# Mixture of experts in the order of token counts, with two-pass down products for the smallest four

## Chip, cores and metric

The kernel runs on one core of a Trainium2 chip. The metric is the device time of one execution in microseconds (us). Three executions of the kernel before gave 1408.19 to 1408.69, median 1408.42.

## What is computed

A decoder trunk of two layers on 256 tokens of 1024 channels, in float32. Layer 0 is a pooling mixer and a dense SwiGLU; layer 1 is a gated DeltaNet and a top-2-of-8 mixture of expert SwiGLUs, each with a hidden width of 3584. The change is within the experts alone:

```python
top_vals, top_idx = lax.top_k(logits, TOP_K)
top_w = jax.nn.softmax(top_vals, axis=-1)
gates = jnp.sum(jax.nn.one_hot(top_idx, N_EXPERTS) * top_w[..., None], axis=1)
for e in range(N_EXPERTS):
    y = swiglu(t, w_gate[e], w_up[e], w_down[e])
    out = out + gates[:, e:e + 1] * y
```

`swiglu` is `(silu(x @ w_gate) * (x @ w_up)) @ w_down`. Run with its drawn inputs, the reference sends 53, 51, 58, 82, 64, 88, 44 and 72 tokens to experts 0 to 7.

## The kernel before

**Splitting.** Every float32 operand is split into a rounded part and a remainder: ScalarE (ACT) casts the rounded part (`whi`, `xgh`, `th`), VectorE (DVE) subtracts it from the source to get the remainder (`wlo`, `xgl`, `tl`). A product is three TensorE (PE) matmuls that add into one PSUM bank: hi by hi, hi by lo and lo by hi.

**Weights.** The experts' weights lie in memory in units of 1 MB (`in_moe`, 42 units per expert, in the order of use). The SyncE queue (SP) loads them into a ring of 16 buffers (`raw`, `raw_s`, `raw_t`); each unit is split in two halves by `half`, with four buffers each for `whi` and `wlo`.

**Jobs.** `expert_steps` writes the jobs out: for each expert seven chunks of 512 hidden columns, each with eight gate and up jobs (6 matmuls of 512 columns each) and four down jobs (6 matmuls each, in `down_mm`) for the chunk before. `moe_pass` runs them: ahead of job i it issues the split of job i+3 (`ahead`), then the job's matmuls, then what hangs on it: `turn` (transposes the 128x512 hidden tile and splits it into `th` and `tl`), `opened` (silu), `gated` (the product with the up half) and `put` (copies the finished rows and writes them to memory by an indirect DMA). Each engine keeps the order in which its instructions were written, since `Lane.__getattr__` (line 200) records them; so nearly every row of the profile has line 200, and the tile names tell the rows apart.

**Tokens.** `choose` builds one-hot matrices `Sp` for two experts of 128 rows each from their ranks `rf`, and `gather` multiplies the tokens with them, 8 groups of 4 matmuls of 256 columns, each group followed by two copies out of PSUM (`xgh`, `xgl`). This is done for a pair of experts at a time, between the jobs of the expert ahead. `opening` is the start of the stage: it computes the first gate product on all tokens while the router's `pick` and `ranks` run on DVE. If an expert has more than 128 tokens, a second pass (`moe_pass(1)`) follows; the test for it stands at the end (lines 1685 and 1686).

Of the kernel before, what the change touches and what calls it, by code (L numbers as in the profile page):

```python
# [52 lines left out]
TURN = 4  # L53
SWAP = 9
# [157 lines left out]
def trunk(ctx: ExitStack, tc, x, gcol, win, prm, bc, cst, eye, pre, moe, out):  # L212
# [1020 lines left out]
    state, sel, xg, yps = {}, {}, {}, {}  # L1233
# [25 lines left out]
    m1, m2, ed, den, w1, w2 = [sm(n_, 1) for n_ in ("m1", "m2", "ed", "den", "w1", "w2")]  # L1259
# [4 lines left out]
    cmi = cmi[:, :1]  # L1264
# [43 lines left out]
    def ranks():  # L1308

        prk = ms_bank([P, 2, 8])  # L1310
        pe.matmul(prk[:, 0, :], ber, mk[:, 0, :], start=True, stop=True)
        pe.matmul(prk[:, 1, :], ber, mk[:, 1, :], start=True, stop=False)
        pe.matmul(prk[:, 1, :], onr, mk[:, 0, :], start=False, stop=True)
        dve.scalar_tensor_tensor(rf, prk, 1.0, mk.bitcast(F32), op0=ALU.add, op1=ALU.mult)

        pn = ms_bank([P, 8])
        for tt in range(2):
            pe.matmul(pn, onr, mk[:, tt, :], start=tt == 0, stop=tt == 1)
        return pn

    def most(pn):

        cmx = mp.tile([P, 1], F32, name="cmx")
        dve.tensor_reduce(cmx, pn, axis=AX.X, op=ALU.max)
        dve.tensor_copy(cmi, cmx)
# [14 lines left out]
    def choose(pr_):  # L1340
        Sp = state["mp"].tile([P, 2, 2, P], F32R, name="Sp", bufs=1)
        for tt in range(2):
            for k in range(2):
                dve.tensor_scalar(Sp[:, tt, k, :], iota[:, :P], rf[:, tt, 2 * pr_ + k:2 * pr_ + k + 1], None,
                                  op0=ALU.is_equal)
        state["Sp", pr_] = Sp
        for k in range(2):
            xg[2 * pr_ + k] = [None, None]

    def gather(pr_, kc, lo_eng=None, bank_=None):  # L1350
        if kc % 4 == 0:
            t = xg_tiles(kc // 4)
            for k in range(2):
                xg[2 * pr_ + k][kc // 4] = t
        pg = (bank_ or ms_bank)([P, 2, 256])
        for i, src in enumerate((hh, hl)):
            for tt in range(2):
                pe.matmul(pg[:, i, :], src[:, tt, kc * P:(kc + 1) * P],
                          state["Sp", pr_][:, tt].rearrange("p a b -> p (a b)"), start=tt == 0, stop=tt == 1)
        for i in range(2):  # L1360
            (dve.tensor_copy if i and lo_eng else act.copy)(xg[2 * pr_][kc // 4][i][:, kc % 4, :], pg[:, i, :])

    def back(e):
        pst = ms_bank([P, 2, P])
        for tt in range(2):
            pe.matmul(pst[:, tt, :], state["Sp", e // 2][:, tt, e % 2, :], idr, start=True, stop=True)
# [3 lines left out]
    def where(e):  # L1370

        pw = ms_bank([P, 8])
        for tt in range(2):
            pe.matmul(pw, state["Sp", e // 2][:, tt, e % 2, :], tid[:, tt, :], start=tt == 0, stop=tt == 1)
        spare = econ[:, 6:7]
        dve.scalar_tensor_tensor(spare, pw[:, e:e + 1], 0.0, econ[:, 3:4], op0=ALU.is_equal, op1=ALU.mult)
        dve.tensor_tensor(slot[:, e:e + 1], spare, pw[:, e:e + 1], op=ALU.add)

    def put(e, q):
        if q == 0:  # L1380
            state["put"] = state["rows"].tile([P, D], F32, name="rows", bufs=2)
        act.copy(state["put"][:, HQ[q]], yps[e][q])
        if q == 1:
            pool.indirect_dma_start(kept_rows, bass.IndirectOffsetOnAxis(ap=slot[:, e:e + 1], axis=0), state["put"], None)
# [12 lines left out]
    def opened(pg):  # L1397
        hm = row_tile()
        act.activation(hm, pg, AF.Silu)
        return hm  # L1400

    def gated(hm, pu_):
        dve.tensor_mul(hm, hm, pu_)
# [8 lines left out]
    def hidden_T(hm, spare):  # L1412
# [7 lines left out]
    def gate_pick():  # L1420

        ps_ = ms_bank([P, 512])
        for i in range(2):
            for tt in range(2):
                pe.matmul(ps_, state["Sp", 0][:, tt, 0, :], state["first"][i][tt], start=i == tt == 0, stop=i == tt == 1)
# [3 lines left out]
    def last_mm(e, c, part):  # L1429

        y, (th, tl), (hi, lo) = yps[e], state["hid", e, c], part
        for q in range(2):
            for a, b in ((th, hi), (tl, hi), (th, lo)):
# [272 lines left out]
```

## Time and profile before

| | |
|---|---|
| median of 3 runs | 1408.42 us |
| the profiled execution | 1407.77 us |
| span of its profile, first to last instruction | 1405.8 us |
| PE busy | 1384.8 us, 99% of the span |
| DVE busy | 1177.8 us, 84% |
| ACT busy | 1004.0 us, 71% |
| memory read | 420.11 MB |
| expert stage | from about 419 us to 1393 us of the span |

Times in the rows are us from the start of the span. A matmul's duration is from its first read to its modelled end; the engine starts the next one earlier, so the distance between two starts is what a matmul costs.

### The profile page before, as it was taken

The numbers are of one execution on the slowest core, as the hardware profiler recorded it, in microseconds if no ns is written. First come the engines' busy times: TensorE is split into PE (matmuls) and PEld (weight loads), VectorE is DVE, ScalarE is ACT, GpSimd is POOL, SyncE is SP. The second block draws the span as 40 slices with busy tenths as digits, with TensorE's granted clock in tenths as the row PEclk, the third lists the DMA queues.
The fourth block names the chain that finished last, engine by engine and source line by source line (L and its number), as shares of the span: only waits on it lengthen the run. The fifth ranks groups of instructions, "written<-read, shape, count | busy, mean of one in ns | idle before, by whom it ended". The sixth has DMA issues, their size and how long they took to land.

```text
span 1405.8 us, 19741 instructions
## 1 busy us (share of the span) xinstructions
PE 1384.8 (99%) x7399; PEld 1186.5 (84%) x7399; DVE 1177.8 (84%) x1438; ACT 1004.0 (71%) x1322; POOL 66.3 (5%) x73
## 2 busy tenths in 40 slices
PE   8999999999999999999999999999999999999996
PEld 8999998989988888888888888888888888888875
DVE  5655556687888999998899999899999989999996
ACT  5544445753566777878877887887887788778775
POOL 0000001121330000000000000000000000000001
PEclk9999999999999999999999999999999999999998
DMA  9465552633159999999999999899999999997880
GB/s 381 156 219 193 180 180 113 263 114 122 65 205 420 364 374 371 397 376 365 357 375 377 378 390 378 332 385 376 372 377 382 368 341 383 375 368 298 334 353 32
DMA packets 61123, 428.24 MB, mean 305 GB/s; under 512 B 6880, under 2 KB 7136, under 8 KB 10592
## 3 DMA queue, kind: packets, MB, share of 16 engines
q1 hardware_dynamic: 59584, 422.75, 78.1%
q0 software_dynamic: 1008, 3.67, 0.7%
q8 instruction: 59, 0.97, 0.3%
q10 hardware_dynamic: 432, 0.53, 0.1%
q14 instruction: 40, 0.33, 0.1%
HBM read 420.11 MB, written 6.82 MB: 304 GB/s over the span
## 4 chain that ended last, share of the span: by engine, by line
PE 94%; DVE 3%; ACT 1%; issue 1%; POOL 0%; DMA 0%; POOLq 0%; SPq 0%; DVEq 0%; ACTq 0%
PE gu L200 59%; PE y L200 21%; PE ya L200 9%; DVE wlo L200 2%; PE yq L200 2%; PE ms L200 1%; PE tp L200 1%; PE gs L200 1%; ACT whi L200 0%; DVE h L200 0%; DMA h<-in_x 0%; DVE xl L200 0%; ACT xh L200 0%; DVE raw L200 0%; POOL raw L200 0%
## 5 line engine op out<-in xcount | busy, mean ns | idle before, releaser
L200 DVE TENSOR_TENSOR wlo<-raw,whi 128x1024 fp32r<-128x1024 f32 x345 | 417.1, 1227 | 92.5 <-ACT whi L200 81.9
L200 DVE TENSOR_TENSOR wlo<-raw_s,whi 128x1024 fp32r<-128x1024 f32 x378 | 456.4, 1223 | 40.6 <-ACT whi L200 22.0
L200 ACT CAST whi<-raw_s 128x1024 fp32r<-128x1024 f32 x378 | 396.5, 1056 | 81.2 <-PE gu L200 45.4
L200 ACT CAST whi<-raw 128x1024 fp32r<-128x1024 f32 x346 | 359.4, 1053 | 110.0 <-PE gu L200 65.2
L200 PE MATMUL gu<-whi,xgh 128*128 128x512 f32 x896 | 355.6, 397 | 0.0
L200 PE MATMUL gu<-wlo,xgh 128*128 128x512 f32 x896 | 349.5, 390 | 0.5 <-DVE wlo L200 0.5
L200 PE MATMUL gu<-whi,xgl 128*128 128x512 f32 x896 | 349.6, 390 | 0.0
L200 PEld LDWEIGHTS gu<-whi,xgl 128*128 128x128 f32 x896 | 168.2, 188 | 36.6
L200 PEld LDWEIGHTS gu<-wlo,xgh 128*128 128x128 f32 x896 | 168.4, 188 | 34.2 <-DVE wlo L200 1.3
L200 PEld LDWEIGHTS gu<-whi,xgh 128*128 128x128 f32 x896 | 168.3, 188 | 32.9
L200 PE MATMUL y<-whi,th 128*128 128x512 f32 x440 | 171.4, 390 | 0.0
L200 PE MATMUL y<-wlo,th 128*128 128x512 f32 x440 | 171.3, 389 | 0.0
L200 PE MATMUL y<-whi,tl 128*128 128x512 f32 x440 | 135.5, 389 | 0.0
L200 PEld LDWEIGHTS y<-whi,tl 128*128 128x128 f32 x440 | 82.6, 188 | 17.2
L200 PEld LDWEIGHTS y<-wlo,th 128*128 128x128 f32 x440 | 82.6, 188 | 16.7
L200 PEld LDWEIGHTS y<-whi,th 128*128 128x128 f32 x440 | 82.6, 188 | 16.8
L200 PE MATMUL gu<-xh,wlo 128*128 128x256 f32 x320 | 90.0, 281 | 0.8 <-DVE wlo L200 0.8
L200 PE MATMUL gu<-xh,whi 128*128 128x256 f32 x320 | 90.1, 281 | 0.1
L200 PE MATMUL gu<-xl,whi 128*128 128x256 f32 x320 | 89.9, 281 | 0.0
L200 PEld LDWEIGHTS gu<-xh,wlo 128*128 128x128 f32 x320 | 61.3, 192 | 1.0 <-DVE wlo L200 1.0
L200 PEld LDWEIGHTS gu<-xh,whi 128*128 128x128 f32 x320 | 60.2, 188 | 0.7 <-ACT whi L200 0.3
L200 PEld LDWEIGHTS gu<-xl,whi 128*128 128x128 f32 x320 | 60.1, 188 | 0.3
(375 smaller groups left out, 1650.8 us busy)
## 6 DMA issues: line engine op xcount, KB each, us to landing
raw_s<-in_moe SPq DMA_DIRECT2D x189, 1024.0 KB, 6.7
raw<-in_moe SPq DMA_DIRECT2D x126, 1024.0 KB, 6.7
raw<-in_pre SPq DMA_DIRECT2D x56, 1024.0 KB, 5.0
raw_t<-in_moe SPq DMA_DIRECT2D x20, 1024.0 KB, 6.6
rows<-AB SPq DMA_DIRECT2D x2, 1024.0 KB, 5.5
raw<-rows SPq DMA_DIRECT2D x2, 1024.0 KB, 7.3
gbc<-in_bc SPq DMA_DIRECT2D x3, 512.0 KB, 7.8
h<-in_x SPq DMA_DIRECT2D x2, 512.0 KB, 3.9
```

What stands on the lines that cost most here:

```text
L200: r = f(*a, **k)
```

## The change

Expert 0 stays first; the other seven follow by falling token count, and their weights are loaded from unit numbers that are read into registers (`first_unit`). Experts 0 and 1 of this order run as before. Then a test on `fit`, the larger of two numbers, twice the count at the fifth place and the largest count of all, chooses one of two programs for the remaining six: if `fit` is at most 128, the last four experts have 64 rows each and share one `choose` and one `gather`, their hidden tile has 64 rows, and its transpose is stored as one tile of 128 columns, 64 rounded and 64 remainders. One matmul of this tile with `whi` and one with `wlo` then give the product's two parts in rows 0 to 63 and 64 to 127, which `put` adds. The other program is the old one for six experts, with the test for a second pass at its end.

```diff
+FEW, SLIM = 4, 64
     def ranks():
+        pn = ms_bank([P, 8])
+        for tt in range(2):
+            pe.matmul(pn, onr, mk[:, tt, :], start=tt == 0, stop=tt == 1)
...
+        dve.memset(key[:, 0:1], 1.0e6)
+        dve.scalar_tensor_tensor(key[:, 1:], pn[:, 1:], float(NE), iota[:, P + 1:], op0=ALU.mult, op1=ALU.add)
+        dve.tensor_tensor(ge, key[:, None, :].to_broadcast([P, 8, 8]), key[:, :, None].to_broadcast([P, 8, 8]), op=ALU.is_ge)
+        dve.tensor_reduce(place, ge, axis=AX.X, op=ALU.add)
...
         dve.scalar_tensor_tensor(rf, prk, 1.0, mk.bitcast(F32), op0=ALU.add, op1=ALU.mult)
+        sorted_(rf)
+        yield
...
+        dve.scalar_tensor_tensor(fit, some[:, NE - FEW:NE - FEW + 1], float(P // SLIM), top, op0=ALU.mult, op1=ALU.max)
...
     def hidden_T(hm, spare, n=P):
         tp = gu_bank((P, 4, P))
         for k in range(4):
-            pe.transpose(tp[:, k, :], hm[:, k * P:(k + 1) * P], C("ident"))
+            pe.transpose(tp[:, k, :n], hm[:n, k * P:(k + 1) * P], C("ident")[:n, :n])
+        if n < P:
+            state["side"] = 1 - state.get("side", 0)
+            th = pair(True)[0] if spare else state["tmp"].tile([P, 4, P], F32R, name=("th", "tl")[state["side"]], bufs=1)
+            split(th[:, :, :n], th[:, :, n:], tp[:, :, :n])
+            return th, None
...
             pe.matmul(y[q], th[:, fc, :], hi[:, HQ[q]], start=st, stop=False)
-            pe.matmul(y[q], th[:, fc, :], lo[:, HQ[q]], start=False, stop=False)
-        for q in qs:
+            pe.matmul(y[q], th[:, fc, :], lo[:, HQ[q]], start=False, stop=sp_ and tl is None)
+        for q in qs if tl is not None else ():
             pe.matmul(y[q], tl[:, fc, :], hi[:, HQ[q]], start=False, stop=sp_)
...
+        n, r, y = width(e), state["put"], yps[e][q]
+        if n == P:
+            act.copy(r[:, HQ[q]], y)
+        else:
+            act.copy(r[:n, HQ[q]], y[n:2 * n])
+            dve.tensor_add(r[:n, HQ[q]], r[:n, HQ[q]], y[:n])
...
-                        after(at + (3, 5)[q], put, e, q)
+                        after(at + (3, 3 if e == 1 else 5)[q], put, e, q)
...
+                if (e, c) == (2, 0) and not block:
+                    after(len(jobs) - 3, turn, *prev)
+                    down(*prev)
+                    prev, cut = None, len(jobs)
...
+            if start:
+                choose(range(2, 4))
+                ahead(start)
+                for kc in range(KC):
+                    gather(range(2, 4), kc, dve)
+                    if kc % 4 == 3:
+                        ahead(start + 1 + kc // 4)
...
+        fv = nc.values_load(fit[0:1, 0:1], min_val=0, max_val=2 * T)
+        with tc.If(fv <= P) as arm:
+            fresh()
+            units.clear()
+            steps_ = expert_steps(block, FEW)
+            run(cut, len(steps_[0]))
+        with arm.Else():
...
-            if i == len(jobs) - 20 and block == 0:
-                tc.mark_branch_hint_location("rest", "LikelyTaken", [mybir.EngineType.PE, mybir.EngineType.DVE,
...
-    rv = nc.values_load(cmi[0:1, 0:1], min_val=0, max_val=T)
-    with tc.If(rv > P, label="rest"):
-        moe_pass(1)
```

The order of instructions at three places follows.

**PE, the down jobs.** Before, one job of any expert (`y_4744` and `y_4745` are the two banks of the result):

```order
L200 MATMUL y_4744<-whi,th 128x512
L200 MATMUL y_4744<-wlo,th 128x512
L200 MATMUL y_4745<-whi,th 128x512
L200 MATMUL y_4745<-wlo,th 128x512
L200 MATMUL y_4744<-whi,tl 128x512
L200 MATMUL y_4745<-whi,tl 128x512
```

Now, one job and the first row of the next, in one of the last four experts:

```order
L203 MATMUL y_10065<-whi,th 128x512
L203 MATMUL y_10065<-wlo,th 128x512
L203 MATMUL y_10066<-whi,th 128x512
L203 MATMUL y_10066<-wlo,th 128x512
L203 MATMUL y_10065<-whi,th 128x512
```

The two matmuls with `tl` are gone. The gate and up jobs keep their six.

**ACT, where expert 1 ends.** Before, the copies of its rows stand among the splits for expert 2:

```order
L200 CAST whi<-raw_s_6748 128x1024
L200 COPY rows<-y_5772 128x512
L200 CAST whi<-raw_s_6748 128x1024
L200 CAST whi<-raw 128x1024
L200 COPY rows<-y_5773 128x512
L200 CAST whi<-raw 128x1024
```

Now:

```order
L203 CAST whi<-raw 128x1024 x3
L203 COPY rows<-y_5798 128x512
L203 COPY rows<-y_5799 128x512
L1692 TENSOR_LOAD cmi
L1693 COMPARE_AND_BRANCH
L203 CAST whi<-raw_s_6640 128x1024
L203 CAST xgh_6646<-ms 128x256 x4
L203 CAST whi<-raw_s_6640 128x1024
L203 CAST xgh_6680<-ms 128x256 x4
L203 CAST whi<-raw_s_6710 128x1024 x2
```

Both copies, the load of the tested number and the branch now stand ahead of the first split of expert 2 and of its gather, on every engine; SP has issued the loads up to here and goes on by itself.

**DVE, the router's ranks in the opening.** Before:

```order
L200 SCALAR_TENSOR_TENSOR rf<-ms,mk 128x16
L200 TENSOR_SCALAR Sp<-iota,rf 128x128 x4
L200 TENSOR_REDUCE cmx<-ms 128x1
L200 CAST cmi<-cmx 128x1
L200 TENSOR_TENSOR wlo<-raw,whi 128x1024
L200 TENSOR_TENSOR tl<-gu,th 128x512
```

Now, up to the split that follows the one-hot matrices:

```order
L203 MEMSET raw 128x1
L203 SCALAR_TENSOR_TENSOR raw<-ms,iota 128x7
L203 TENSOR_TENSOR raw<-raw 128x64
L203 TENSOR_REDUCE raw<-raw 128x8
L203 TENSOR_TENSOR raw<-raw,iota 128x64
L203 SCALAR_TENSOR_TENSOR rf<-ms,mk 128x16
L203 TENSOR_TENSOR raw<-raw,rf 128x64 x2
L203 TENSOR_REDUCE rf<-raw 128x16
L203 TENSOR_SCALAR Sp<-iota,rf 128x128 x4
L203 TENSOR_TENSOR wlo<-raw,whi 128x1024
```

Seven small operations and a memset come ahead of `Sp`. Behind this `wlo`, and ahead of `tl`, fifteen more stand where two stood: those of `ranks` after its first `yield`.

## Rows read from the trace of the kernel before

**Rows 1.** The page: busy us, share of the span, instructions.

```profile
PE 1384.8 (99%) x7399; PEld 1186.5 (84%) x7399; DVE 1177.8 (84%) x1438; ACT 1004.0 (71%) x1322; POOL 66.3 (5%) x73
```

**Rows 2.** Stretches: window; length, busy us of engines, PE's clock, DMA share, GB/s.

```profile
550.00:600.00 50.00, 50.00 (x228) 41.35 (x227) 46.25 (x43) 40.97 (x44) 1.55 (x1) 1.00 1.00 392
1300.00:1350.00 50.00, 49.76 (x225) 40.80 (x224) 47.43 (x44) 39.32 (x42) 0.00 (x0) 1.00 0.88 359
```

**Rows 3.** Waits between 460 and 1380 us: total us, times, longest.

```profile
DVE wlo L200 <- ACT whi L200: 37.9, 123, 1.2
PE gu L200 <- DVE wlo L200: 0.5, 2, 0.2
```

**Rows 4.** Timeline of POOL, the writes of finished rows: start, duration, idle before.

```profile
690.27 1.35 POOL L200 DMA_INDIRECT rows<-rows,cmi  x1 [120.32 <-ACT rows L200]
808.22 1.36 POOL L200 DMA_INDIRECT rows<-rows,cmi  x1 [116.59 <-ACT rows L200]
930.12 1.36 POOL L200 DMA_INDIRECT rows<-rows,cmi  x1 [120.54 <-ACT rows L200]
```

**Rows 5.** Timeline of PE: two gate jobs, then two down jobs, begin here.

```profile
599.99 0.39 PE L200 MATMUL gu<-whi,xgh 128*128 128x512 f32 x1
...
601.35 0.39 PE L200 MATMUL gu<-whi,xgh 128*128 128x512 f32 x1
...
610.00 0.39 PE L200 MATMUL y<-whi,th 128*128 128x512 f32 x1
...
611.36 0.39 PE L200 MATMUL y<-whi,th 128*128 128x512 f32 x1
```

**Rows 6.** Timeline of DVE and ACT in the same chunk.

```profile
605.33 0.69 DVE L200 TENSOR_TENSOR tl<-gu,th 128x512 fp32r<-128x512 f32 x1
606.63 2.00 ACT L200 CAST whi<-raw 128x1024 fp32r<-128x1024 f32 x2
607.71 2.36 DVE L200 TENSOR_TENSOR wlo<-raw,whi 128x1024 fp32r<-128x1024 f32 x2 [0.21 <-ACT whi L200]
611.13 0.68 DVE L200 TENSOR_TENSOR hm<-hm,gu 128x512 f32<-128x512 f32 x1
```

**Rows 7.** SP's waits; a weight load's time to landing; the stretch where the ring fills.

```profile
SPq L200 <- DVE wlo L200: 917.7, 329, 20.0
...
raw_s<-in_moe SPq DMA_DIRECT2D x189, 1024.0 KB, 6.7
...
444.00:448.00 4.00, 4.00 (x19) 3.28 (x18) 2.51 (x3) 2.78 (x5) 0.00 (x0) 1.00 1.01 428
```

**Rows 8.** Timeline of DVE and PE in the opening.

```profile
430.60 0.18 DVE L200 SCALAR_TENSOR_TENSOR l<-o,lg 128x16 f32<-128x16 f32 x1
...
433.25 0.17 DVE L200 SCALAR_TENSOR_TENSOR rf<-ms,mk 128x16 f32<-128x16 f32 x1 [1.18 <-PE ms L200]
433.46 0.88 DVE L200 TENSOR_SCALAR Sp<-iota,rf 128x128 fp32r<-128x128 f32 x4
...
436.13 0.40 PE L200 MATMUL ms<-Sp,hnh 128*128 128x256 f32 x2
...
436.60 0.40 PE L200 MATMUL ms<-Sp,hnh 128*128 128x256 f32 x2
...
437.68 0.76 DVE L200 CAST xgl<-ms 128x256 fp32r<-128x256 f32 x2 [1.35 <-ACT xgh L200]
...
438.49 0.39 PE L200 MATMUL gu<-whi,xgl 128*128 128x512 f32 x1
```

**Rows 9.** ACT's queue at the test of the kernel before: duration ns, start us.

```profile
L1685 ACTq TENSOR_LOAD <-cmi x1: 1068/1068/1068, 1400.5 to 1400.5; - x1
...
L1686 ACTq EVENT_SEMAPHORE  x1: 17/17/17, 1402.1 to 1402.1; - x1
```

**Rows 10.** The tile of finished rows: ACT's copies, ns.

```profile
L200 ACT COPY rows<-y x14: 579/587/589, 565.0 to 1287.1; 128x512 f32<-128x512 f32 x14
```

**Rows 11.** A stretch, as in rows 2, right after the last matmul.

```profile
1396.00:1400.00 4.00, 0.00 (x0) 0.00 (x0) 2.76 (x8) 2.97 (x8) 2.64 (x4) 0.78 0.07 27
```

More of the change, by code (lines that the diff above doesn't have):

```diff
@@ L1313, in ranks @@
         pe.matmul(prk[:, 1, :], onr, mk[:, 0, :], start=False, stop=True)
-        dve.scalar_tensor_tensor(rf, prk, 1.0, mk.bitcast(F32), op0=ALU.add, op1=ALU.mult)
[L1316 to L1325, printed above, removed]
+        b, at = raw_tile(), [0]
@@ L1558, in expert_steps, with fresh @@
         down(*prev)
-        return jobs, post
+        return jobs, post, cut
+    def fresh():
+        for lane in (pe, act, dve, pool, sp):
+            lane.last = None
     def moe_pass(block):
-        jobs, post = expert_steps(block)
-        parts_, loads, n = {}, {}, [0]
+        parts_, loads, n, units, stop = {}, {}, [0], {}, [0]
         def take(u, s, lo_eng=None):
+            e, i = u
             if s == 0:
-                loads[u] = load(moe, u, 2 if u == NE * UPE - 1 else 1)
+                if e and e not in units:
+                    units[e] = nc.sync.value_load(first_unit[0:1, e:e + 1], min_val=0, max_val=(NE - 1) * UPE)
+                loads[u] = load(moe, units[e] + i if e else i, 2 if u == (NE - 1, UPE - 1) else 1)
@@ L1568, in take, with run @@
             return half(loads[u], s, lo_eng)
         def ahead(k, lo_eng=None):
-            while n[0] <= min(k, len(jobs) - 1):
-                u, s, _ = jobs[n[0]]
+            while n[0] <= min(k, stop[0] - 1):
+                u, s, _ = steps_[0][n[0]]
                 parts_[n[0]] = take(u, s, lo_eng)
                 n[0] += 1
-        if block == 0:
-            opening(take, ahead, post)
-        else:
+        def run(start, end):
+            jobs, post, _ = steps_
+            stop[0] = end
+            if start:
[5 more added lines that the diff above has]
+                        ahead(start + 1 + kc // 4)
+            for i in range(start, end):
+                last = i >= len(jobs) - SWAP
+                if i == len(jobs) - 5:
+                    state["g"] = raw_tile()[:, :D]
+                    sp.dma_start(state["g"], bc[4:5, :].to_broadcast([P, D]))
+                if (block or i > 1) and not last:
+                    ahead(i + 3)
+                jobs[i][2](parts_.pop(i))
+                for f in post.pop(i, ()):
+                    f()
+                if last:
+                    ahead(i + 3)
+            if end == len(jobs):
+                for i in sorted(post):
+                    for f in post[i] if i >= start else ():
+                        f()
@@ L1600, in moe_pass @@
-        for i in sorted(post):
-            for f in post[i]:
-                f()
+            return run(0, len(steps_[0]))
+        cut = stop[0] = steps_[2]
+        opening(take, ahead, steps_[1])
+        run(0, cut)
+        every = [state, sel, xg, yps, cols, parts_, loads, units, ring]
+        saved = [{k: (list(v) if isinstance(v, list) and d is xg else dict(v) if k == "width" else v) for k, v in d.items()}
+                 for d in every]
+        at = n[0]
+        fv = nc.values_load(fit[0:1, 0:1], min_val=0, max_val=2 * T)
@@ new lines, in moe_pass @@
+        with tc.If(fv <= P) as arm:
[4 more added lines that the diff above has]
+        with arm.Else():
+            for d, d_ in zip(every, saved):
+                d.clear()
+                d.update(d_)
+            fresh()
+            units.clear()
+            n[0] = at
+            steps_ = expert_steps(block)
+            run(cut, len(steps_[0]))
+            rv = nc.values_load(cmi[0:1, 0:1], min_val=0, max_val=T)
+            with tc.If(rv > P):
+                fresh()
+                moe_pass(1)
+            fresh()
@@ L1604, in opening @@
+        fresh()
     def opening(take, ahead, post):
```

162 lines of the change are left out of this document (97 added, 65 removed).

## The prediction

> **What bounds the kernel now.** I read the page first: PE is busy for 99% of the span [rows 1]. Since a busy PE can still be one that is fed late, I then read the stretches and the waits of the expert stage. Between 550 and 600 us PE is busy for all 50 us, DVE for 46.25, ACT for 40.97 [rows 2]. Between 460 and 1380 us PE waited for a `wlo` 0.5 us in all [rows 3]. So PE sets the pace of the stage, and DVE stands right behind it, at 92%.
>
> The timeline gives the pace. The writes of finished rows lie 808.22 - 690.27 = 117.95 us apart where no gather falls between them and 930.12 - 808.22 = 121.90 where one does [rows 4]: an expert costs PE 117.95 us and a gather 3.95. Two jobs of six matmuls begin 1.36 us apart, gate jobs and down jobs alike [rows 5], so a matmul costs 0.227 us.
>
> **The change, part by part.**
>
> *Which program runs.* The reference's counts, with expert 0 first, sort to 53, 88, 82, 72, 64, 58, 51, 44. The fifth is 64, so `fit` is the larger of 2 x 64 and 88, which is 128, and the test asks for at most 128. It holds, with not one token to spare, and the last four experts run in 64 rows.
>
> *Down products in two passes.* Each of the four experts loses 7 chunks x 4 jobs x 2 matmuls = 56 matmuls, 56 x 0.227 = 12.7 us of PE, and would take PE 117.95 - 12.7 = 105.2 us. DVE's work hardly falls. In a chunk it does 12 `wlo` at 1.18 (two in 2.36), one `hm` of 0.68 and one `tl` of 0.69 [rows 6]: 15.5 us, in seven chunks 108.7, which is 92% of 117.95 and agrees with the busy time above. Of this only `tl` shrinks, to half its columns. The trace has no such subtraction; a copy of 256 columns takes 0.38 [rows 8] and the full one 0.69, and I take 0.4, since the columns are halved. `put` adds two additions of 64x512 per expert, at most 0.68 each like `hm`. So DVE needs 7 x (14.16 + 0.68 + 0.40) + 1.4 = 108.1 us per expert, more than PE's 105.2: the bound passes from PE to DVE. Within a chunk the same is seen job by job: a down job of four matmuls takes PE 0.91 us, while its split takes DVE 1.18; in four down jobs DVE loses 1.1 us, and with `hm` and `tl` another 1.1, and in eight gate and up jobs of 1.36 it wins back 8 x 0.18 = 1.4. I take 108 us, a gain of 10 per expert, **40 us** for four. The ends: 50.8 if more than two `wlo` in a row come closer together than the 1.18 of a pair, so that PE still sets the pace; and 17 if DVE gets no busier than the 47.43 of 50 us that it shows at its fullest [rows 2], 108.1 / 0.95 = 113.8 us. I take the middle because that fullest stretch is one in which PE held it back.
>
> The weights must then come at 44.04 MB per 108 us, 408 GB/s. Row by row: while the ring fills, the queue moved 428 GB/s at a share of 1.01 [rows 7]; in steady state 392 at a share of 1.00 [rows 2], and there SP spent 917.7 us waiting for buffers to be freed by DVE [rows 7], so it was the demand that ended there. Besides, the ring runs ahead: 16 units, less 2.4 in flight (6.7 us to landing, a unit used every 2.81) and two being split, are some 12 MB. Four experts need 176.2 MB in 432 us; even 392 GB/s bring 169, and with the 12 that is enough. I take 0. The Trainium skill, "DMA: Bandwidth & Descriptors", in its section on where 436 GB/s comes from, says that for loads from memory a limit of some 358 GB/s per core binds. The rows of 392 and 428 contradict it here; what it would give is the third rival.
>
> *One gather less.* The last four experts are gathered together, so of three gathers two are left: **-4.0 us** (3.95), on PE, in a stretch that PE bounds. The extra `Sp` columns are the same 256.
>
> *The cut behind expert 1.* Formerly this transition cost only its gather, since expert 2's jobs covered the rest. Now the jobs end, each engine loads `fit` and branches, and the gather stands alone. SP comes there some 16 units early, so loads go on; DVE is about three jobs ahead and has its `Sp` ready. ACT is the late one: both copies of rows stand ahead of its branch and need PE's last matmul (time 0). Two copies, 1.2 us [rows 10]; from load to the instruction after the branch 1402.1 - 1400.5 = 1.6 [rows 9]; the first `whi`, 1.0 [rows 6]: 3.8 us. Then eight groups pass through two banks, each PE 0.47 (436.13 to 436.60), an ACT copy and a DVE copy of 0.38 [rows 8], 1.23 us around for two banks, so a group every 0.62 to 0.65, 5.2 us, and one split of 1.2 stands in between: the first job starts near 10.2. Of this 3.8 us are the matmuls of the gather, which were paid before as well. PE so loses about 6.5 us. Its clock may fall in the pause: in the four us behind the last matmul it was granted 0.78 [rows 11]; I add 1.5 for jobs at the lower of its two levels. **+8 us**. Ends: 4 if test and copies overlap PE's last matmuls; 15 if the clock stays down for several jobs or the arm's instructions come late, for which no row of this trace has a price in mid-program.
>
> *The opening.* DVE gets 8 small operations ahead of `Sp` and 13 more behind the next `wlo` (15 for 2). One takes 0.18 to 0.22 (four `Sp` in 0.88) [rows 8]. Four of the first wait for the same matmuls for which `rf` waits, so `Sp` starts some 1.3 us later, ends near 435.6, and PE needs it at 436.13: covered. Then `wlo` to 436.8, 15 x 0.21 = 3.2 to 440.0, `tl` to 440.6, and the first `xgl` is there at 441.0. It is needed at 438.49 by the third matmul of the first gathered job [rows 8]. DVE's pause of 1.35 ahead of `xgl` is already used in this. **+2.7 us** (1.5 to 4). The work behind it has no cover either, since PE was full there; it moves as a whole.
>
> *The end.* The old test at the end goes; the new arm's jump stands in its place. Both lie beside the last writes' landing: 0, at most +2. The matmuls that turn `Sp` around for the last expert: +0.5.
>
> **Sum.** -40 - 4 + 8 + 2.7 + 0.5 = -32.8. The profiled execution took 1407.77 us, 0.65 less than the median of the runs: 1408.4 - 32.8 = **1376 us** (rounded). A difference of 0.2%, 2.8 us, is what the measurement can tell from none.
>
> **Rivals.**
>
> 1. *PE keeps the pace.* If DVE closes its gaps, the gain is 50.8 and the time 1365 (1358 to 1367). For it: the 1.18 holds the tail of a pair's second row, so a long series may run faster. Against: in the down jobs its split is 0.27 us longer than PE's job. Chance 0.14.
>
> 2. *The cut costs much more.* All five engines enter code behind a test without a hint. By the rows above the test is 1.6 us, of which 1.07 is the load [rows 9], so the branch took some 0.5; but that one had a hint, which is taken out. If each entry stalls and the clock stays low, 15 to 25 us in place of 8: 1383 to 1393. The Trainium skill, "Runtime: NRT & Kernel Launch", section on instruction fetch, says that a taken branch to a target outside the loaded window waits for a DMA fetch; no row here shows one without a hint, nor whether this arm is entered by a jump. Chance 0.13.
>
> 3. *The weights arrive late.* If the queue cannot go beyond the 373 GB/s that today's pace asks for (44.04 MB in 117.95 us), four experts lack 176.2 - 161 - 12 = 3 MB, 8 us: 1384. A second form, a limit near the 359 GB/s of the slower stretch [rows 2], would lack 9 MB, 26 us: 1402, nearly the old time; 392 in 50 us [rows 2] speaks against it. The skill's rule above names 358 and is this second form. Chance 0.10, of which 0.02 for the second form.
>
> 4. *The test fails: slower.* Were the fifth count 65, `fit` would be 130 and the old program would run, with the cut (8) and the opening (2.7) and no gain: 1419. The point is one token: 64 against 65. For it: nothing is to spare, and the router's sums are made of split products. Against: the counts come from logits whose second and third places differ by 0.003 or more for every token, by the reference. Chance 0.05.
>
> **Chances and range.** The forecast, DVE as the bound (1367 to 1385), has the remaining 0.58. The range of 1362 to 1392 leaves out the fourth rival, the low end of the first and the top of the second and third, together about 0.16. Faster by over 0.2%: all but the fourth rival and the edge of the third, 0.94. Within 0.2%: 0.01. Slower: 0.05.
>
> **What would show it.** Right: the writes of rows of the last experts lie near 108 us apart; there DVE is busy for 48 us or more of 50, and PE waits for `wlo`; 224 fewer matmuls in all; 390 to 410 GB/s; a pause of PE, broken by gather matmuls, of some 10 us behind expert 1, with ACT's copies and branch ahead of it; PE waiting some 2.7 us for `xgl` in the opening. Wrong: distances of 105 (PE leads), of 114 (DVE saturates below full), SP or ACT waiting for transfers of `in_moe`, a second gap on entry into the arm, or six matmuls in every down job to the end.

## The result, and the profile after

The changed kernel took 1382.66 us (median of four runs, 1381.82 to 1386.19) against 1408.44 of the kernel before beside it: ratio 0.982, 95% interval 0.980 to 0.984. In a second set of five runs it took 1384.21 (1382.10 to 1385.62), ratio 0.983 (0.981 to 0.984). Forecast were 1376 and a range of 1362 to 1392: faster, inside the range, and 25.8 us won where 32.4 were forecast. The profiled execution took 1383.05 us, its span 1381.3.

The page after, first line (before: [rows 1]):

```profile
PE 1349.6 (98%) x7149; PEld 1065.4 (77%) x7149; DVE 1171.3 (85%) x1473; ACT 983.0 (71%) x1298; POOL 114.4 (8%) x73
```

PE's busy time fell by 35.2 us, its share by one point only: it now waits in places. Stretches and waits of the kernel after, which answer to [rows 2] and [rows 3] (length, busy us of PE, PEld, DVE, ACT, POOL, PE's clock, DMA share, GB/s; then total us, times, longest):

```profile
1100.00:1150.00 50.00, 50.00 (x223) 30.74 (x222) 48.15 (x47) 41.20 (x47) 0.00 (x0) 1.00 1.00 406
1200.00:1250.00 50.00, 50.00 (x221) 31.46 (x220) 48.19 (x47) 41.91 (x46) 0.00 (x0) 1.00 1.01 412
```

```profile
PEld gu L203 <- DVE wlo L203: 15.5, 29, 1.6
PEld y L203 <- DVE wlo L203: 8.6, 30, 0.8
```

DVE is at 48.2 of 50 us where it was at 46.25, and PE's weight loads now wait for `wlo` (24 us; before, 1.3 for `gu`). From one write of rows to the next DVE is busy for 105.1 of 108.4 us. The rest are short waits for `whi`, the only ones that it has there; this stretch, then its waits from 1055.65 to 1272.48, which is two experts:

```profile
1055.65:1164.08 108.43, 108.35 (x478) 66.91 (x476) 105.10 (x101) 91.11 (x101) 17.33 (x2) 1.00 1.00 409
```

```profile
DVE wlo L203 <- ACT whi L203: 6.5, 35, 0.2
```

A busy PE of 50.00 does not show this, since a matmul's duration covers small gaps; the distance between like rows does. A good mark is the transpose of a hidden tile, once in a chunk. Timeline of PE after, these rows in the last expert:

```profile
1287.70 0.46 PE L203 MATMUL gu<-idr,hm 64*128 64x64 f32 x4
1303.14 0.46 PE L203 MATMUL gu<-idr,hm 64*128 64x64 f32 x4
1320.48 0.46 PE L203 MATMUL gu<-idr,hm 64*128 64x64 f32 x4
1337.82 0.46 PE L203 MATMUL gu<-idr,hm 64*128 64x64 f32 x4
```

The second transpose of each expert, in both traces, gives the account of the whole stage:

| mark (second transpose) | before | after | later by | what lies between |
|---|---|---|---|---|
| expert 1 | 587.25 | 593.72 | 6.47 | the opening |
| expert 2 | 709.39 | 722.98 | 13.59 | the cut: +7.1 |
| expert 3 | 827.10 | 840.68 | 13.58 | nothing |
| expert 4 | 949.25 | 961.71 | 12.46 | expert 3 ends, 4 begins: -1.1 |
| expert 5 | 1066.96 | 1070.87 | 3.91 | -8.6 |
| expert 6 | 1189.12 | 1179.29 | -9.83 | -13.7, a gather of 3.95 in it |
| expert 7 | 1306.82 | 1287.70 | -19.12 | -9.3 |
| end of the span | 1405.8 | 1381.3 | -24.5 | -5.4 |

So the opening cost 6.5 us (forecast 2.7) and the cut 7.1 (8). The rest, 38.1, is the gather and the two passes together. With the gather at its forecast 4.0 the two passes brought 34.1, where 39.5 were forecast: 40, less 0.5 for the matmuls that turn `Sp` around. (By the marks of the kernel before, a stretch with a gather is 122.2 - 117.7 = 4.5 us longer, so the split between the two is good to half a us.) A full expert takes 108.4 us, 15.45 a chunk; but in the last one two chunks take 17.34.

Three places of the trace after show where. First the opening, timeline of DVE, then of PE:

```profile
436.12 1.22 DVE L203 TENSOR_TENSOR wlo<-raw,whi 128x1024 fp32r<-128x1024 f32 x1
437.25 0.16 DVE L203 COPY raw<-ms 128x8 f32<-128x8 f32 x1
...
437.71 1.94 DVE L203 TENSOR_TENSOR raw<-raw 128x64 f32<-128x64 f32 x1
...
441.92 0.68 DVE L203 TENSOR_TENSOR tl<-gu,th 128x512 fp32r<-128x512 f32 x1
442.52 0.74 DVE L203 CAST xgl<-ms 128x256 fp32r<-128x256 f32 x2
```

```profile
437.46 0.52 PE L203 MATMUL ms<-Sp,hnh 128*128 128x256 f32 x2 [0.29 <-DVE raw L203]
...
442.75 0.47 PE L203 MATMUL gu<-whi,xgh 128*128 128x512 f32 x1 [3.58 <-DVE tl L203]
...
443.29 0.40 PE L203 MATMUL gu<-whi,xgl 128*128 128x512 f32 x1
...
445.57 0.63 PE L203 MATMUL ms<-Sp,hnl 128*128 128x256 f32 x2
```

The first matmul of the first gathered job waits 3.58 us for `tl`, which reads the bank `gu` that the job writes. Fifteen small operations stand ahead of `tl`, and one of them took 1.94 us in place of 0.22. The first `xgl`, for which the third matmul would have waited, is there at 442.9 (half of the 0.74 behind 442.52), right behind `tl`; without the wait for `tl` the third matmul could have begun at most 0.4 us sooner. Behind the pause PE's clock is at its lower level, 1.2 GHz: the pair that takes 0.40 elsewhere takes 0.63, and the stretch from 444 to 446 was granted 0.53.

Second the cut, the chain of waits of the kernel after (start, us, what):

```profile
679.40 0.59 ACT rows L203
...
680.40 1.05 ACT whi L203
...
681.48 1.22 DVE wlo L203
...
683.09 2.09 PE ms L203 x8
...
685.47 1.06 ACT whi L203
...
686.55 1.23 DVE wlo L203
...
688.16 1.21 PE ms L203 x8
689.37 6.91 PE gu L203 x30
```

From the copy of rows to the first job it is 10.0 us (forecast: 10.2 from PE's last matmul), and it is a relay of ACT, DVE and PE. The test takes next to no part in it: ACT's first split begins 0.2 us behind the end of its two copies, and its load of the tested number (0.48 us, from 679.6) ran beside them. Twice a `whi` and a `wlo` stand ahead of the copies that PE needs for the next groups of the gather.

Third the last expert, timeline of PE, the waits only, and of DVE:

```profile
1314.35 0.44 PE L203 MATMUL gu<-wlo,xgh 128*64 128x512 f32 x1 [1.14 <-DVE wlo L203]
1317.81 0.45 PE L203 MATMUL gu<-wlo,xgh 128*64 128x512 f32 x1 [0.49 <-DVE wlo L203]
```

```profile
1311.89 1.27 DVE L203 SCALAR_TENSOR_TENSOR h<-raw,six,h 128x1024 f32<-128x1024 f32 x1
...
1315.36 1.27 DVE L203 SCALAR_TENSOR_TENSOR h<-raw,six,h 128x1024 f32<-128x1024 f32 x1
```

These are the sums of the finished rows with `h` (`gain`), two in each of the two slow chunks. The kernel before has the same four sums in the same two chunks. Its marks there:

```profile
1323.64 0.60 PE L200 MATMUL gu<-idr,hm 128*128 128x128 f32 x4
1341.03 0.60 PE L200 MATMUL gu<-idr,hm 128*128 128x128 f32 x4
1358.38 0.60 PE L200 MATMUL gu<-idr,hm 128*128 128x128 f32 x4
```

That is 17.39 and 17.35 us a chunk, where its other chunks take 16.82. So the sums cost 1.1 us before, and the same chunks are 3.8 us longer than their neighbours now.

But there was a second suspect, on POOL and in the stretches around the last write of rows:

```profile
943.91 1.33 POOL L203 DMA_INDIRECT rows<-rows,cmi  x1 [120.76 <-ACT rows L203]
...
1272.48 17.32 POOL L203 DMA_INDIRECT rows<-rows,cmi  x1 [91.09 <-DVE rows L203]
```

```profile
1275.00:1285.00 10.00, 9.90 (x43) 6.27 (x42) 10.00 (x11) 8.14 (x9) 10.00 (x1) 1.00 0.00 0
1325.00:1335.00 10.00, 8.53 (x36) 5.28 (x34) 9.85 (x9) 7.48 (x8) 0.00 (x0) 1.00 1.01 425
```

The write of 64 rows holds POOL for 17.3 us, that of 128 rows 1.33. The fetch of the finished rows waits for the last one in SP's queue, and for more than 10 us no weight is loaded (0 GB/s). Late weights would explain the new part just as well.

### The profile page after: what moved, and what is told of

Read it like the earlier page. It is cut to its first block, busy times and chain, and to the rows that moved or that the text cites. A ratio compares the mean times of both kernels' runs of the same rounds, so it can differ in the third digit from the quotient of the medians.

```text
span 1381.3 us, 19930 instructions
## 1 busy us (share of the span) xinstructions
PE 1349.6 (98%) x7149; PEld 1065.4 (77%) x7149; DVE 1171.3 (85%) x1473; ACT 983.0 (71%) x1298; POOL 114.4 (8%) x73
## 4 chain that ended last, share of the span: by engine, by line
PE 89%; DVE 6%; issue 2%; ACT 1%; POOL 1%; DMA 0%; SPq 0%; ACTq 0%; POOLq 0%; DVEq 0%
PE gu L203 59%; PE y L203 17%; PE ya L203 9%; DVE wlo L203 4%; PE yq L203 2%; PE tp L203 1%; PE ms L203 1%; ACT whi L203 1%; PE gs L203 1%; DVE raw L203 0%; DVE h L203 0%; DVE rows L203 0%; DMA h<-in_x 0%; DVE hm L203 0%; DVE xl L203 0%
## 5 line engine op out<-in xcount | busy, mean ns | idle before, releaser
L203 PE MATMUL gu<-whi,xgh 128*128 128x512 f32 (+1 forms) x896 | 356.0, 397 | 3.6 <-DVE tl L203 3.6
L203 PE MATMUL gu<-wlo,xgh 128*128 128x512 f32 (+1 forms) x896 | 352.4, 393 | 3.2 <-DVE wlo L203 3.2
L203 PE MATMUL gu<-whi,xgl 128*128 128x512 f32 (+1 forms) x896 | 351.5, 392 | 0.0
L203 PEld LDWEIGHTS gu<-wlo,xgh 128*128 128x128 f32 (+1 forms) x896 | 144.9, 162 | 69.2 <-DVE wlo L203 15.5
L203 PEld LDWEIGHTS gu<-whi,xgh 128*128 128x128 f32 (+1 forms) x896 | 144.8, 162 | 60.5 <-issue 3.9
L203 PEld LDWEIGHTS gu<-whi,xgl 128*128 128x128 f32 (+1 forms) x896 | 144.8, 162 | 58.0
L203 PE MATMUL y<-wlo,th 128*128 128x512 f32 x328 | 128.9, 393 | 0.5 <-DVE wlo L203 0.3
L203 PE MATMUL y<-whi,th 128*128 128x512 f32 x328 | 128.4, 391 | 0.2 <-ACT th L203 0.2
L203 POOL DMA_INDIRECT rows<-rows,cmi x7 | 57.2, 8165 | 792.4 <-ACT rows L203 499.8
L203 PE MATMUL y<-whi,tl 128*128 128x512 f32 x336 | 113.1, 391 | 0.0
L203 PEld LDWEIGHTS y<-whi,th 128*128 128x128 f32 x328 | 61.6, 188 | 13.7 <-ACT th L203 0.6
```

The lines of the kernel that those rows point to most:

```text
L203: r = f(*a, **k)
```

## The experiments

The theories of each run stand in the text that was on record before it.

### Who sets the pace in the last four experts

**One pass.**

```diff
-            pe.matmul(y[q], th[:, fc, :], hi[:, HQ[q]], start=st, stop=False)
-            pe.matmul(y[q], th[:, fc, :], lo[:, HQ[q]], start=False, stop=sp_ and tl is None)
+            pe.matmul(y[q], th[:, fc, :], hi[:, HQ[q]], start=st, stop=sp_ and tl is None)
+            if tl is not None:
+                pe.matmul(y[q], th[:, fc, :], lo[:, HQ[q]], start=False, stop=False)
```

> In the last four experts the matmul of th with wlo is left out of the down products too (this leaves out the products of the hidden tile with the weights' remainders there), so that a down job has two matmuls; the splits stay. Theory A (DVE sets the pace of 108.4 us per expert): the distance between the writes of rows stays at 108 to 108.5 us, and the last expert does not get faster either; the span falls by less than 2 us. Theory B (PE sets it, with 12.7 us per expert in these matmuls): the distance falls by 10 us or more, toward 96, and the span by 40 us.

One run, 1389.51 us. The writes of rows lie 1166.47 - 1058.00 = 108.47 and 109.97 us apart. Stretch of this run:

```profile
1200.00:1250.00 50.00, 45.35 (x197) 26.24 (x196) 47.96 (x46) 41.73 (x47) 0.00 (x0) 1.00 1.00 412
```

PE loses 12.7 us of work per expert and the pace does not get faster; PE waits instead (27.5 us for `wlo` at `gu` between 1060 and 1340). So PE's work does not set the pace, and Theory B fell. That DVE's work does, the next run and the sums left out show from the other side. The time even rose. In two stretches of 10 us behind 1300, among longer pauses, PE's clock was granted 0.83 and 0.85; how much of the rise this is, one run cannot tell.

**Part of the splits on POOL** (with full rows written, as below).

```diff
-                parts_[n[0]] = take(u, s, lo_eng)
+                parts_[n[0]] = take(u, s, pool if width(u[0]) < P and n[0] % 12 == 0 and u[1] > 7 and n[0] < len(steps_[0]) - 12 else lo_eng)
```

> In the last four experts one split of twelve has its wlo on POOL in place of DVE, in six chunks of each expert (and full rows are written, so that POOL is not held by the write). Theory A (DVE alone sets the pace of 108.4 us): DVE is relieved of some 6 x 1.18 = 7 us per expert, PE's 105.2 binds, the distance between the writes of rows falls to 105 to 106, and the time by 9 to 12 us, to about 1372. Theory B (POOL's tensor operations hold DVE's up): the distance stays at 108 or rises, and the wlo beside POOL's take well over 1.18 us.

1410.82 us (eleven runs, 1408.47 to 1413.01), ratio to the kernel before 1.002 (1.001 to 1.003): the whole gain of the change is gone. POOL took one split in each chunk, seven of an expert rather than six, and the chunk grew from 15.45 to 16.36 us. POOL, then DVE:

```profile
1101.43 2.41 POOL L203 TENSOR_TENSOR wlo<-raw,whi 128x1024 fp32r<-128x1024 f32 x1 [13.96 <-ACT whi L203]
```

```profile
1102.54 2.39 DVE L203 TENSOR_TENSOR wlo<-raw,whi 128x1024 fp32r<-128x1024 f32 x1 [1.41 <-ACT whi L203]
1104.85 1.21 DVE L203 TENSOR_TENSOR wlo<-raw_s,whi 128x1024 fp32r<-128x1024 f32 x1
```

POOL works from 1101.43 to 1103.84; DVE's split that begins beside it is done 1.09 us after POOL's end, where one alone takes 1.21. DVE does not share, it waits. Spared one split, it first stood 1.41 us for the next `whi`, and then lost 1.2 us behind POOL: nothing was won, and each chunk lost 0.9. Theory B. The Trainium skill, "SBUF — State Buffer", section on the two separate sides, says that VectorE and GpSimd share a pair of ports as an exclusive lock: an operation of VectorE with two inputs in SBUF and one of GpSimd that reads SBUF exclude each other for the whole instruction. These rows agree.

### What the last expert lost

**Full rows.**

```diff
+        if n < P:
+            dve.tensor_copy(slot[n:, e:e + 1], econ[n:, 3:4])
...
             act.copy(r[:n, HQ[q]], y[n:2 * n])
+            act.copy(r[n:, HQ[q]], y[n:])
...
-            pool.indirect_dma_start(kept_rows, bass.IndirectOffsetOnAxis(ap=slot[:n, e:e + 1], axis=0), r[:n], None)
+            pool.indirect_dma_start(kept_rows, bass.IndirectOffsetOnAxis(ap=slot[:, e:e + 1], axis=0), r, None)
```

> The last four experts write all 128 rows of their tile (rows 64 to 127 to spare rows) in place of 64. Theory A (the 64-row indirect write holds POOL for 17.3 us, and the fetch of finished rows waits for the last one in SP's queue ahead of the last expert's loads): POOL's write falls to about 1.4 us, SP's wait for the rows from 29.7 to about 12 us, the empty stretch of the weight queue at 1270 to 1290 shrinks, the last expert no longer waits for wlo at 1310 to 1340, and the time falls by about 3 us, to 1379.7. Theory B (the weights are late in the last expert because the queue cannot carry 408 GB/s plus the fetched rows): POOL may be quicker, the waits stay, the time is the same within 1 us. The extra copies cost ACT 0.6 us four times twice, which B would show as up to 1 us more.

1383.85 us (1381.96 to 1385.21), ratio to before 0.983 (0.982 to 0.984): no different from the kernel after. POOL's write fell to 3.96 us, SP's wait for the rows from 29.7 to 16.2, and the weights ran ahead again:

```profile
1275.00:1285.00 10.00, 9.93 (x43) 6.25 (x42) 10.00 (x11) 8.54 (x9) 0.63 (x1) 1.00 0.73 278
1325.00:1335.00 10.00, 8.39 (x36) 5.27 (x35) 9.84 (x10) 7.43 (x8) 0.00 (x0) 1.00 1.01 423
...
1345.00:1355.00 10.00, 10.00 (x46) 5.82 (x46) 9.81 (x10) 8.25 (x11) 0.00 (x0) 1.00 0.04 15
```

All weights have landed by 1345, more than 10 us sooner than in the kernel after, and PE's gap at 1325 is as before. The empty stretch of the queue, striking as it is, cost nothing: the ring covered it. Theory A fell here, and B with it, since the weights were not late at all.

**The sums on POOL.**

```diff
-        dve.scalar_tensor_tensor(h[:, tt], state["kept", k][:, tt], (w1, w2)[k][:, tt], h[:, tt], op0=ALU.mult, op1=ALU.add)
+        r = state["kept", k][:, tt]
+        pool.tensor_tensor(r, r, (w1, w2)[k][:, tt].to_broadcast([P, D]), op=ALU.mult)
+        pool.tensor_tensor(h[:, tt], r, h[:, tt], op=ALU.add)
```

> The sum of the finished rows with h (four operations of 128x1024 in chunks 3 and 4 of the last expert) goes from DVE to POOL, as a product and a sum. Writing full rows brought the last expert's weights 13 us sooner, and PE's gaps at 1305 to 1335 stayed, so late weights are not their cause. Theory A (the four operations of DVE, which by now sets the pace, cost their own time there): PE's gaps in these stretches go, and the time falls by 4 to 5 us, to 1378. Theory B (POOL and DVE hinder each other on the same memory, as one small operation of DVE took 1.94 us in place of 0.22 beside POOL's split in the opening): DVE's wlo take longer than 1.18 us while POOL works, and the time falls by less than 2 us or rises.

1393.20 us (1392.35 to 1394.36), ratio 0.990 (0.988 to 0.991), some 10 us slower than the kernel after. DVE:

```profile
1317.95 12.92 DVE L203 TENSOR_TENSOR wlo<-raw_s,whi 128x1024 fp32r<-128x1024 f32 x5
```

Five splits beside POOL's sums take 12.92 us, where five in a row took 5.75 a little earlier (from 1299.35). There it was POOL that stood: its first product, begun at 1298.05, has a span of 8.80 us, the next ones 2.8 to 2.9. Theory B again; what the sums cost on DVE this run cannot tell.

**The sums left out.** Hence the direct way:

```diff
-        dve.scalar_tensor_tensor(h[:, tt], state["kept", k][:, tt], ...
+        dve.scalar_tensor_tensor(h[:, tt, :1], state["kept", k][:, tt, :1], ...
```

> The four sums of finished rows with h in the last expert are cut to one column each (this leaves out the other 1023 columns of those sums). On POOL they held DVE's wlo up, so that run could not tell their own price on DVE. Theory A (the last expert's smaller gain is DVE's time for these sums, 4 x 1.27 us, in a stretch that DVE bounds): PE's waits for wlo of 1.14, 0.49, 1.13 and 0.48 us at 1314 to 1335 go, the stretch from the last write of rows to the end shrinks by about 3.2 us, and the time is near 1380. Theory B (the loss has another place, such as the fetch itself or late weights): the waits stay, and the stretch shrinks by less than 1 us.

1381.03 us (1380.31 to 1382.05). From 1305 to 1345 PE is busy for 39.87 of 40 us, and the slow chunks are gone:

```profile
1303.91 0.46 PE L203 MATMUL gu<-idr,hm 64*128 64x64 f32 x4
1319.49 0.46 PE L203 MATMUL gu<-idr,hm 64*128 64x64 f32 x4
1335.08 0.46 PE L203 MATMUL gu<-idr,hm 64*128 64x64 f32 x4
```

15.58 and 15.59 us a chunk against 17.34: 3.5 us. From the last write of rows to POOL's first operation of the end it is 1368.36 - 1273.24 = 95.12, against 1371.12 - 1272.48 = 98.64. Theory A. The medians differ by less than that (1.6 to 3.2 us, by the set of the kernel after), the spans of the two profiled runs by 2.8, since the first write of rows came 0.7 us later here (575.59 against 574.86).

### The opening

**Ranks behind job 2.**

```diff
-        next(rk_)
         gate_rows(0)
...
+        post.setdefault(2, []).append(lambda: next(rk_))
```

> The second part of the ranks (15 operations of DVE) is moved from ahead of the split tl of the first hidden tile to behind job 2. Theory A (PE's pause of 3.6 us at 439 to 442.75 is its wait for tl, which frees the bank gu, and the clock falls after that pause): the wait goes, the clock stays at 1.00, expert 0 ends some 5 us earlier (near 566.5 in place of 571.4), the time falls by 4 to 6 us, to about 1378. Theory B (the pause is the first gathered job's wait for xgl, as the prediction had it): the same fall, but before this the wait in the kernel after should have named xgl. Theory C (what costs is DVE being held while POOL works on its own wlo, wherever the small operations stand, or there is no slack for them behind job 2 either): at most 2 us are gained, and waits of PE for wlo appear behind 445.

1382.62 us (1381.26 to 1383.59), ratio 0.982 (0.980 to 0.983): no gain to be measured. The pause for `tl` went, and the clock stayed at 1.00, but two others came:

```profile
438.95 0.51 PE L203 MATMUL ms<-Sp,hnh 128*128 128x256 f32 x2 [1.40 <-DVE xgl L203]
443.63 0.52 PE L203 MATMUL ms<-Sp,hnh 128*128 128x256 f32 x2 [1.15 <-DVE xgl L203]
```

The first copy of expert 0's rows came at 570.05, 1.4 us earlier than in the kernel after (571.43). Theory C in part. A likely reason lay in the edit: the copy of the counts out of PSUM had moved as well, so one of the two banks `ms` was held and the gather ran on the other alone.

**Ranks behind job 12**, with that copy left in the first part.

```diff
+        dve.tensor_copy(cnt, pn)
         yield
...
-        dve.tensor_copy(cnt, pn)
...
-        post.setdefault(8, []).append(weights)
+        post.setdefault(12, []).append(lambda: next(rk_))
+        post.setdefault(16, []).append(weights)
         for k in range(2):
-            post.setdefault(9 + k, []).append(lambda k=k: where(k))
+            post.setdefault(17 + k, []).append(lambda k=k: where(k))
```

> The second part of the ranks goes behind job 12, the weights of the tokens behind job 16, the slots behind jobs 17 and 18; only the copy of the counts stays in the first part, so that its bank is free for the gather (moving all of it behind job 2 took away PE's pause of 3.6 us and the fall of the clock, but PE then waited 1.4 and 1.2 us for xgl, because that copy came late and a bank was held by it, and the time was the same). Theory A (that held bank, and DVE being full until 460, gave the gain back): no wait of PE over 0.6 us between 430 and 450, expert 0's first copy of rows near 567 in place of 571.4, the time about 1378.5, ratio to the kernel after 0.997. Theory B (the late start comes from the ring of weights, which lends a buffer to the ranks, and from PE's matmuls for the counts): expert 0 ends at 569 to 570 again, the time within 1.5 us of the kernel after.

1378.65 us (1377.99 to 1380.42), ratio 0.979 (0.978 to 0.981). Between 430 and 460 PE is busy throughout; the first copy of rows is at 566.72, 4.7 us earlier. Theory A; which of the two brought it, the early copy or the late place of the rest, the run does not tell apart. Of the opening's 6.5 us some 1.8 are left (by the transpose of expert 1, 589.01 - 587.25), among them:

```profile
464.55 0.50 PE L203 MATMUL gu<-wlo,xgh 128*128 128x512 f32 x1 [1.03 <-DVE wlo L203]
```

### The cut

**No test.** The edit takes out the test and the `Else` program, builds the steps with `expert_steps(block, FEW)` from the start, and puts expert 2's gather back among expert 1's jobs.

> No test and no second program: experts in the same order, the slim program in one piece, expert 2's gather among expert 1's jobs and its splits ahead as in the kernel before. It leaves out the program for counts that do not fit. Theory A (the cut costs the drained pause alone, by the marks of the experts' ends 7.1 us): 1382.7 - 7 = 1375.7, all of it between the ends of experts 0 and 2; the pace of the later experts stays at 108.4. Theory B (code that stands behind a branch also costs on the way, by instruction fetch in every expert, or at the end jump): more than 9 us are gained, with a pace below 108.4 or an earlier end. Theory C (the cut is mostly paid back, since the ring of weights fills in the pause): under 4 us are gained.

1374.63 us (1374.02 to 1378.32), ratio 0.977 (0.976 to 0.978), 8.0 us less than the kernel after in its first set, 9.6 less than in its second. Expert 3's rows are written at 936.85 in place of 943.91, 7.06 us earlier; another 1.4 us come at the end, where no jump stands (from POOL's first operation of the end to the end of the span 8.8 us, against 10.2). The pace between the writes is 108.4 still. Theory A in the main: the cut is a pause, and code behind a test costs nothing on the way. Of Theory B only the jump at the end is seen, with these 1.4 us.

**Gather first.**

```diff
-                ahead(start)
-                for kc in range(KC):
+                for kc in range(6):
+                    if kc == 4:
+                        ahead(start)
                     gather(range(2, 4), kc, dve)
-                    if kc % 4 == 3:
-                        ahead(start + 1 + kc // 4)
...
+                for kc in (6, 7) if start and i == start else ():
+                    gather(range(2, 4), kc, dve)
```

> In the arm the first four groups of the gather stand ahead of the first split of expert 2 on ACT and DVE, two more behind it, the last two behind the first job. Theory A (the pause of 9.8 us is a chain of ACT and DVE: PE waits 2.55 us for an xgl that stands behind a wlo, which waits for whi): the first job begins some 6 to 7.5 us after expert 1's last matmul, and the time falls by 2.5 to 4 us, to about 1379.5. Theory B (the pause is set by the test and the entry into the arm, or by PE's clock, which falls in it anyway): within 1 us of the kernel after. Slower by 1 to 2 us if the splits of the second and third job come late now, which would show as waits for wlo behind the first job.

1381.46 us (1380.67 to 1381.79), ratio 0.981 (0.980 to 0.982). PE's longest wait in the pause fell from 2.55 us to 0.76, and expert 2's write came at 819.75 in place of 821.79. Theory A, with 2.0 us, a little under its size; two waits of 0.76 for `wlo` in the first jobs stand against it. PE's clock was granted 1.00 in each stretch of 2 us from 680 to 696, where the kernel after had 0.50 from 684 to 686, so a part of the 2.0 is the clock; how large, the run does not tell.

**The other program.** The test asks for at most 1:

```diff
-        with tc.If(fv <= P) as arm:
+        with tc.If(fv <= 1) as arm:
```

> The test asks for at most 1 in place of 128, so that the other program runs: the old one for six experts, behind a taken branch. Theory A (the late opening, 6.5 us, and the cut, 7.1 us, are all that the change costs, and the second gather is back): 1408.1 + 13.6 = 1421.7, with 117.95 us between the writes and 121.9 where a gather falls, and the pause behind expert 1 as long as in the kernel after. Theory B (a jump to the far program costs more than falling into the near one, in the fetch of instructions): 1425 or more, with a pause behind expert 1 longer than that of the kernel after by the difference, in which no engine waits for data.

1427.58 us (1427.13 to 1427.69), ratio 1.014 (1.012 to 1.015). The chain of waits at the cut, and PE's branch (duration, start):

```profile
679.86 0.11 ACT rows L203
679.97 4.34 issue
```

```profile
L1693 PEldq COMPARE_BRANCH  x1: 5997/5997/5997, 678.0 to 678.0; - x1
```

Here the branch is taken, and ACT, DVE and PE each stand 4.0 to 4.8 us without waiting for any data; in the kernel after, where the arm follows the test, ACT's split stood right behind its copies. PE's clock is then at 0.50 from 682 to 694. From expert 0's write to expert 2's it is 827.02 - 574.58 = 252.4 us, against 246.9 in the kernel after and 239.8 before. Theory B, though only for the program that is jumped to. The Trainium skill, "Runtime: NRT & Kernel Launch", section on instruction fetch, names such a stall for a taken branch whose target is not loaded; these rows agree with it, and the kernel after, which falls through, shows that the near arm goes free.

**The kernel after, again.**

> The kernel after, unchanged, for a paired time: 1382 to 1383 us, and in the profile the wait of PE for tl at 439 to 443, with the fall of the clock behind it, is there again.

1384.21 us, and the wait for `tl` is there (3.62 us at 443.08). This profile is of a run of 1385.62 us. Its cut, and that of the kernel after (1383.05), a stretch of each:

```profile
690.00:692.00 2.00, 2.00 (x7) 1.71 (x7) 0.88 (x3) 1.52 (x4) 0.00 (x0) 0.50 0.95 397
```

```profile
686.00:688.00 2.00, 0.99 (x7) 0.78 (x5) 1.48 (x3) 1.23 (x3) 0.00 (x0) 0.89 0.00 0
```

Both have 0.50 from 684 to 686. In the first the clock is at its lower level until 692, in the second it rises before 688 (mean 0.89). Up to the gather's second wait the two traces lie 0.35 us apart (688.51 and 688.16), and at a later pair of like rows, with both clocks back, 2.45 (698.56 and 696.11); between the writes of experts 0 and 2 lie 249.1 and 246.9 us. So these 2.1 us, of the 2.6 between the two runs, are the clock in the pause.

### Late ranks and early gather together

> The late ranks (1378.65 us alone) and the gather ahead of the first split (2 us earlier at expert 2's end alone) together. If they are independent: 1376.5 to 1377.5, and the write of expert 2's rows at about 816 in place of 821.8. If the pause behind expert 1 depends on how full the ring of weights is, which the late ranks change too: 1378 to 1379.

1377.26 us (1376.84 to 1378.54), ratio to before 0.978 (0.977 to 0.979), against 0.983 (0.981 to 0.984) of the kernel after in the same set: 7 us less, with both programs kept. Expert 2's write is at 816.56. In the pause PE's clock does not fall, as with the early gather alone:

```profile
682.00:684.00 2.00, 2.00 (x13) 1.78 (x14) 1.60 (x3) 0.42 (x2) 0.00 (x0) 1.00 0.00 0
```

The two are independent, and the runs lie closer together (1.7 us from lowest to highest, 3.5 in the kernel after). From expert 0's write to expert 2's it is 245.0 us still, 5.2 more than before.

## Why the prediction was right, and where its terms were off

*Which program runs.* Right: 250 fewer rows of PE (224 were forecast for the down products; the gather's 32 come to them), and two passes to the end. The fourth rival's price (1419) was too low. Its kernel took 1427.6: the opening cost 3.5 us more than the 2.7 in that price, and the cut 12.6 (252.4 - 239.8) in place of 8. The jump to the far program, which lengthened it, is what the second rival had feared for the near one.

*Two passes.* The step itself held: the bound passes from PE to DVE. One pass less of PE brought nothing, four sums less of DVE brought 3.5 us. But that a sum of 108.1 us met a pace of 108.4 is in part luck. DVE was busy for 105.1 us of an expert. Splits in a row cost less than the 1.18 of a pair (four take 4.61 us at 1125.96 of the kernel after, 1.15 each), as the first rival had it, and by that DVE's work is no more than the 105.2 forecast for PE. The other 3.3 us are DVE's waits for `whi`, which the sum does not have. So the first rival's premise was right, and its conclusion was not: PE did not set the pace. ACT's `whi` in turn waits for PE's `gu` jobs there (25.0 us, 79 times between 1060 and 1270), by the trace; whether more buffers for `whi` would close the gaps no run shows.

What the sum also left out are the four sums of 1.27 us that DVE does in the last expert: it counted DVE's work of a common expert and took it four times. As long as PE set the pace they cost 1.1 us; as soon as DVE does, they cost 3.5, which is 2.4 more. With the pace (4 x 0.4) this is 4.0 of the 5.4 us missing in this term. The other 1.4 stay open, in part because the marks give an expert of the kernel before 117.7 us, where the forecast took 117.95.

*Weights.* Right: 406 to 412 GB/s in the last experts, and the ring bridged even such a gap without a load. The third rival is out, in both its forms.

*The cut.* Right in sum and nearly in parts, 7.1 for 8; in other runs of the same code up to 9.3, by the clock. But of the 1.6 us given to the test at most 0.4 was seen; what took its place were two rounds of ACT, DVE and PE, because the split stood ahead of the gather's copies.

*The opening.* This is the term that was mis-sized, 6.5 us for "+2.7 us", and its path was wrong in one place. The forecast had the third matmul of the first gathered job wait for `xgl`. It was the first matmul, and it waited for `tl`, since `tl` reads the bank that the job overwrites; the forecast knew that `tl` came late (440.6) and did not ask who waited for it. By itself this cost only some 0.3 us, for `xgl` came right behind `tl`. The size lay elsewhere. `xgl` was there at 442.9 and not at 441.0, 1.9 us later: the split ahead began 0.5 us late, and 15 x 0.21 = 3.2 us were in fact 4.7, for one operation stood 1.7 us behind POOL's split (436.51 to 439.57). And the clock fell behind the pause, for which the forecast has no term here: the third matmul (443.29) is 4.8 us later than its like of the kernel before, the job at 447.63, with the clock back, 6.4. That is 1.6, and 0.3 + 1.9 + 1.6 = 3.8 us.

*The end.* 10.2 us from POOL's first operation to the end of the span, 10.7 before: about 0, as forecast; without a test it was 8.8.

Together: opening +3.8, two passes +5.4, cut -0.9, 8.3 us; -32.8 + 8.3 = -24.5, the difference of the spans.

## What to carry to other kernels

When a change hands the bound to another engine, go through all that engine does in the faster stretch, single operations too: what was free under the old bound now has its full price. For each instruction that is made late, list who waits for its operands' banks and buffers, not only for its result. A sum of busy times that meets the measured pace is not yet the pace: ask how much of it the engine was busy, and what it waited for in the rest. A test in mid-program costs least if the likely program follows it directly and the first work behind it is put in the order in which PE needs it (5.2 us here, 7.1 as built); the program that is jumped to pays for the jump (12.6).

## What the chip showed that was not expected

- An indirect write of 64 rows held POOL for 17.3 us in most cases (7.6 in some, 13.9 once) where 128 rows took 1.33 among the full experts and 3.96 in the same place as the 64. Why was not settled.
- DVE and POOL exclude each other: a DVE operation of 0.22 us took 1.94, five splits 12.92 in place of 5.75; once it was POOL's product that took 8.80 in place of 2.8.
- Beside a taken branch, in mid-program, PE's branch took 6.0 us, at the jump behind the last matmul of the kernel after 3.3; where the arm follows the test, 0.1.
- In the pause of some 10 us at the cut PE's clock fell to its lower level, 1.2 GHz. By the granted clock of the stretches it was there for 3.4 us in one run of the kernel after and for 10.2 in another, which made most of the difference between the two. With the gather first, where PE's longest wait there is 0.76 us in place of 2.55, it did not fall.
